# Three edits to the order of work in an encoder block: low parts behind minima, a power behind a weight, another bank for the norm's weights

## The chip, the cores and the metric

The kernel runs on one core of one Trainium2 chip. A core has five engines that run side by side: TensorE (PE, the matmuls, with its weight loads shown apart as PEld), VectorE (DVE), ScalarE (ACT), GpSimd (POOL) and SyncE (SP, which here issues most of the DMAs). Each engine works through its own instructions in the order in which the program holds them; semaphores make one engine wait for another. Matmul results land in PSUM, which has eight banks of 128 partitions x 512 float32; everything else lies in SBUF. The metric is the device time of one execution in microseconds (us), taken as the median of several executions.

## The reference

The program computes one block of an encoder on 1024 tokens of width 1024, with 16 meta tokens ahead of them. All of it is float32:

```python
h = concat([meta, x])                                   # 1040 rows
n = rms_norm(h, norm_mix)                               # y * rsqrt(mean(y*y) + EPS) * gain
qa, ka, va, qb, kb, vb, ga, gb = split(n @ w_in)
y_a = differential_attention(qa, ka, va, ...)           # 4 heads, two softmaxes each, over all keys
y_a = rms_norm(y_a, subln_gain) * (1 - LAMBDA_INIT)     # inside differential_attention, per head
y_b = windowed_gqa(qb, kb, vb, sink_logits)             # 8 heads, keys within 128 tokens and the meta tokens
h = h + (sigmoid(ga) * (y_a @ w_branch_a) + sigmoid(gb) * (y_b @ w_branch_b)) @ w_out
h = h + (silu(f @ w_ff_gate) * (f @ w_ff_up)) @ w_ff_down      # f = rms_norm(h, norm_ffn)
return rms_norm(h, norm_final)[16:]
```

## The kernel before

**Arithmetic.** Nearly every product is made from operands that are split in two: a high part (the value copied into the fp32r type) and a low part (the value minus its high part). A product is then three matmuls: high x high, high x low and low x high. So nearly every matrix that goes into a product needs a copy and a subtraction. Out of PSUM, ScalarE makes the high part (`activation(..., AF.Copy)`) and VectorE the low part (`tensor_tensor(..., ALU.subtract)`); for weights GpSimd makes one or both.

**The stages, in order of time.** First the rows of `x` are normed, turned by TensorE and split into `hT_hi` and `hT_lo`, while the first projections (`kb` and two of `qb`) already run on the columns that are there. Then come the other projections, with the windowed attention ("B") mixed in. From about 268 us the differential attention ("A", lines 1074 to 1161) runs, mixed with the products for the gates (lines 914 to 1031). After that come the two branch products, `w_out`, the feed-forward part and the last norm.

**What sets the order.** A planner orders each engine's instructions by a simulated timeline. Three things bind it. `tc.issue_after(ins)` puts what is written in its block behind `ins` on the engine of `ins`, without a semaphore. `queue_behind` does so for single pairs. And `manual_schedule` keeps the written order: for TensorE from line 1190, for GpSimd from there to line 1226, for all engines in the last stage. So in the first stage, up to about 268 us, TensorE's order too comes from the planner.

**The first stage, around lines 547 to 626.** The weights `norm_mix`, as eight rows of 128, are turned and spread over all partitions by TensorE into two PSUM banks, the list `gain` (lines 560 to 566). The norms of the row tiles 0 and 1 (`norm_x(0, gain)`, `norm_x(1, gain)`) read these banks directly (line 156). For the later tiles the weights are copied into SBUF, `gmix`, by two VectorE copies (`gmix_part`, line 593). Line 549 takes another bank, `idle`, for matmuls on zeros that keep TensorE at work (lines 556 and 569). The banks `pp0`, `pp1` and `pp2` go round (`pp_bank`, line 188): `gain_0` has `pp0`, `gain_1` has `pp1`, the first chunk of `kb` has `pp2`, and then the first chunk of `qb` has `pp0` again. `idle` has the bank `by`, which the windowed attention uses later. The weights of the first `qb` column block are split in `prep` (lines 223 to 230): ScalarE makes the high part (line 224), VectorE one `gmix` half (593), the two halves of the low part (228) and the other `gmix` half (593). Behind the high part ScalarE makes that of a third column block (`q1_h`, line 597), and then squares and sums row tile 2 (line 148, in `norm_x(2)`).

A norm is a chain over three engines: ScalarE squares and sums (148), GpSimd scales the sum and raises it to the power -1/2 (133 and 134), VectorE multiplies by it and by the weights (158). TensorE then turns the result (169), ScalarE and VectorE split it (171 and 173).

**The differential attention.** The loop at line 1200 goes through 32 tiles of 128 queries (4 heads x 8 tiles); a string of slots (line 41) says in which order TensorE gets a piece of the scores ("s"), of the turning of the previous tile ("t"), of the values and the norm ("n"), and a quarter of a gate product ("g"). For each of two softmaxes (`m` = 1, then 0) the scores are made in three chunks (line 1091). The first two lie in the two-bank tile `two`, of which there is one; an instruction on VectorE adds the distances and takes the minimum of both (line 1094, the scores have their sign turned). The third chunk, in one of three banks `sc`, is done by line 1098. ScalarE then takes the exponential (1102), VectorE works out a factor (1105, 1107) and combines both softmaxes (1108). For the tile before, TensorE turns the result in three blocks `b` = 0, 1, 2 (1121), each in a bank `sc`, and each is split by ScalarE (1124) and VectorE (1125).

After every four tiles the values are normed (`normed_a`, 1138): TensorE sums squares (1147), VectorE scales (1151, 1152), GpSimd raises to the power -1/2 (1153), TensorE spreads the factors some slots later (1158).

**The gate products.** `weights_g` (841) makes one operand on GpSimd: for some of them two sums (857, 858), then the copy that is the high part (876) and the subtraction that is the low part (877, kept in the list `made_g`). Each is chained behind the one before. TensorE uses it in four quarters of three matmuls (980). Operands are made up to four products ahead (1031).

Of the kernel before, what the change touches and what calls it, by code (L numbers as in the profile page):

```python
# [79 lines left out]
def encoder_block(ctx: ExitStack, tc: tile.TileContext, x, meta, norm_mix, w_in, lq1, lk1, lq2, lk2,  # L80
# [7 lines left out]
    def f32(ap):  # L88
        return ap.bitcast(F32)
# [13 lines left out]
    def bank(p, tag, name, bufs):  # L103
        return p.tile([P, 512], F32, tag=tag, name=name, bufs=bufs)
# [105 lines left out]
    def prep(col, name, p=None):  # L210
        if col not in raw_w:
            preload(col)
        w = raw_w.pop(col)
        p, bufs = (p, 1) if p else (wpool, W_BUFS)
        wh = p.tile([P, DC, P], F32R, tag="wh", name=f"wh_{name}", bufs=bufs)
        wl = p.tile([P, DC, P], F32R, tag="wl", name=f"wl_{name}", bufs=bufs)
        halves = [slice(4 * b, 4 * b + 4) for b in range(2)]
        if col == C_KB:
            for b in halves:
                nc.gpsimd.tensor_copy(wh[:, b], w[:, b])  # L220
            for b in halves:
                nc.gpsimd.tensor_tensor(wl[:, b], w[:, b], f32(wh)[:, b], ALU.subtract)
        elif col == C_QB:
            high = nc.scalar.activation(wh, w, AF.Copy)
            last = gmix_part(0)
            for b in halves:
                with tc.issue_after(last.ins):
                    last = nc.vector.tensor_tensor(wl[:, b], w[:, b], f32(wh)[:, b], ALU.subtract)
            with tc.issue_after(last.ins):
                gmix_part(1)  # L230
        else:
            split(wh, wl, w, nc.gpsimd)
        return wh, wl
# [312 lines left out]

    zeros = bpool.tile([P, 512], BF16, tag="by1", name="zeros", bufs=2)
    nc.vector.memset(zeros, 0.0)
    idle = bank(psum1, "by", "idle", 1)
    load_x(0)  # L550

    rows = bpool.tile([DC, P], F32, tag="by1", name="gain_rows", bufs=2)
# [6 lines left out]
    nc.vector.tensor_copy(gain_t, pt[:, 0:DC])  # L559
    gain = []  # L560
    for b in range(2):
        pt = pp_bank(f"gain_{b}")
        gain.append(pt)
        for c in range(4):
            k = 4 * b + c
            turned = nc.tensor.transpose(pt[:, c * P:(c + 1) * P], gain_t[:, k:k + 1].broadcast_to([P, P]), ident)
# [21 lines left out]
    q1_h, q1_l = (kvpool.tile([P, DC, P], F32R, tag=tag, name=f"w{tag}") for tag in ("q1", "q0"))  # L588


    def gmix_part(b):
        with tc.issue_after(low.ins):
            return nc.vector.tensor_copy(gmix[:, b * 512:(b + 1) * 512], gain[b])

    with tc.issue_after(highs[-1].ins):
        ensure(2)
        high = nc.scalar.activation(q1_h, w_q1, AF.Copy)
    prepped[C_QB + P] = q1_h, q1_l
    with tc.issue_after(high.ins):
        norm_x(2)  # L600
    with tc.issue_after(normals[-1].ins):
        nc.vector.tensor_tensor(q1_l, w_q1, f32(q1_h), ALU.subtract)
    p_kb = project_steps(C_KB, KB_CHUNKS, "kb", kb_evac, hi_first=True)
# [470 lines left out]
    def scores_a(h, t, ld, s):  # L1074
# [10 lines left out]
        for m in (1, 0):  # L1085
            s[m] = s0s[t % 2] if m == 0 else apool.tile([P, L], F32, tag="s1", name=f"as1_{nm}", bufs=S_BUFS[1])
            two = psum2.tile([P, 2, 512], F32, tag="two", name=f"aps2_{nm}_{m}", bufs=1)
            for i, (k0, n) in enumerate(A_CHUNKS):
                ps = two[:, i] if i < 2 else bank(psum2, "sc", f"aps_{nm}_{m}", SC)
                for vv in range(2):  # L1090
                    nc.tensor.matmul(ps[:, :n], qs[m][:, t * P:(t + 1) * P], ks[m][:, vv, k0:k0 + n],  # L1091
                                     start=(vv == 0), stop=(vv == 1))
                if i == 1:
                    nc.vector.tensor_tensor_reduce(s[m][:, 0:2 * n].rearrange("p (a k) -> p a k", a=2), two[:, :, :n],  # L1094
                                                   dist[:, u0:u0 + 2 * n].rearrange("p (a k) -> p a k", a=2), slope, far_a,
                                                   ALU.add, ALU.min, mn[:, m, 0:1])
# [13 lines left out]
        nc.scalar.copy(more, last)  # L1110
        far_copy(h * NT + t + 2)

    def transpose_a(h, t, s, at_):
        i = t % 2
        for b in range(3):
# [9 lines left out]
            nc.vector.tensor_tensor(lo, pt[:lo.shape[0], :nb], f32(hi)[:lo.shape[0]], ALU.subtract)  # L1125
            yield

    def values_a(h, t, v, at_, py):
# [9 lines left out]
    def normed_a(h, c, py):  # L1138
# [11 lines left out]
        e = small.tile([P, 4], F32, tag="ae", name=f"ae_{nm}", bufs=2)  # L1150
        nc.vector.scalar_tensor_tensor(e, sums, EPS, sums, ALU.mult, ALU.mult)
        nc.vector.scalar_tensor_tensor(f, pst[:, 0:4], 1.0 / P, e, ALU.mult, ALU.add)
        nc.gpsimd.tensor_tensor(f, f, neg_half, ALU.pow)
        for _ in range(N_WAIT):
            yield
        pf = bank(psum2, "sc", f"apf_{nm}", SC)
# [846 lines left out]
```

## Time and profile before

| | us |
|---|---|
| median of the three timed executions | 1407.80 |
| lowest and highest of them | 1406.76 and 1407.81 |
| the profiled execution, device time | 1407.06 |
| its span, first to last instruction | 1405.3 |
| TensorE busy within the span | 1395.5 |
| VectorE busy | 926.8 |
| ScalarE busy | 682.2 |
| GpSimd busy | 661.9 |

The granted TensorE clock was 0.999 over the span. In the profile's timeline a line has the start in us, the duration in us, the engine, the line of the kernel, the operation, its tiles (out<-in), its shape and, in brackets, the idle time of the engine before it with what ended that. The durations of matmuls overlap, because matmuls are pipelined: what TensorE really loses is read from the distance of two starts, beside the usual distance of the same pair. PEld is TensorE's weight load, which runs ahead of the matmul that uses it.

### The profile page before, as it was taken

The page shows a single profiled execution, that of the slowest core. Times are in us where ns is not written, and L with a number is a line of the kernel's source. Part 1 is how long each engine was busy: PE and PEld are TensorE (multiplying, and loading weights), DVE is VectorE, ACT ScalarE, POOL GpSimd, SP SyncE. Part 2 cuts the span into 40 slices and gives each one's busy share as a digit, 9 for nine tenths or more (in the row PEclk, how much of TensorE's full clock was granted, in tenths as well). Part 3 has the DMA queues.
Part 4 walks back from the last instruction along what each step waited for, and adds up shares of the span by engine and source line. Part 5 has one row for each costly group of instructions (what it writes and reads, how often), then busy time and mean ns, then how long its engine had stood idle before and what let it go on. Part 6 is the DMA issues. An engine that isn't in the chain of part 4 may idle for free.

```text
span 1405.3 us, 20672 instructions
## 1 busy us (share of the span) xinstructions
PE 1395.5 (99%) x7169; PEld 1199.8 (85%) x7169; DVE 926.8 (66%) x1594; ACT 682.2 (49%) x1322; POOL 661.9 (47%) x637
## 2 busy tenths in 40 slices
PE   9999999999999999999999999999999999999998
PEld 8989999988888989888888888888888888888886
DVE  7556667676677878657868965644455543887566
ACT  6355565555454656645446644333333333444454
POOL 5347884485686767613404154554455451000442
PEclk9999999999999999999999999999999999999999
DMA  8435658464896363485603534333323324954343
GB/s 235 102 93 169 206 190 285 130 203 137 276 301 219 109 208 106 164 300 165 225 16 140 168 120 146 116 113 113 99 97 112 105 98 135 335 183 142 121 127 143
DMA packets 188601, 226.56 MB, mean 161 GB/s; under 512 B 14584, under 2 KB 122048, under 8 KB 188368
## 3 DMA queue, kind: packets, MB, share of 16 engines
q1 hardware_dynamic: 184736, 219.79, 48.6%
q10 hardware_dynamic: 3760, 5.45, 1.2%
q8 instruction: 57, 0.93, 0.3%
q14 instruction: 48, 0.39, 0.1%
HBM read 152.48 MB, written 68.39 MB: 157 GB/s over the span
## 4 chain that ended last, share of the span: by engine, by line
PE 98%; DVE 1%; ACT 1%; POOL 0%; DMA 0%; issue 0%; ACTq 0%; DVEq 0%; POOLq 0%
PE pg L1765 30%; PE pd L1870 15%; PE pg L980 11%; PE ppa L790 6%; PE aps L1091 4%; PE po L1668 4%; PE apy L1134 3%; PE pp_ka L259 3%; PE pp_va L259 3%; PE pp_qb L259 3%; PE apt L1121 2%; PE bps L449 2%; PE pp_qa L259 2%; PE po L1676 2%; PE bpy L496 1%; PE bpt L490 1%
## 5 line engine op out<-in xcount | busy, mean ns | idle before, releaser
L1765 PE MATMUL pg<-t,wop 128*128 128x512 f32 x1056 | 242.4, 389 | 0.0
L1765 PEld LDWEIGHTS pg<-t,wop 128*128 128x128 f32 x1056 | 198.3, 188 | 41.1
L126 POOL TENSOR_TENSOR wop<-wf,wop 128x512 fp32r<-128x512 f32 x114 | 152.9, 1341 | 162.6 <-ACT wop L125 152.6
L1870 PE MATMUL pd<-ob,oa 128*128 128x512 f32 x924 | 209.6, 389 | 0.0
L1870 PEld LDWEIGHTS pd<-ob,oa 128*128 128x128 f32 x924 | 173.3, 188 | 36.1 <-DVE ob L126 0.2
L1765 PE MATMUL pg<-b,wop 128*128 128x512 f32 x792 | 183.3, 389 | 0.0
L980 PE MATMUL pg<-hT_hi,wopg 128*128 128x512 f32 x488 | 182.1, 400 | 0.3 <-POOL wopg L877 0.3
L1765 PEld LDWEIGHTS pg<-b,wop 128*128 128x128 f32 x792 | 148.5, 188 | 30.7
L125 ACT ACTIVATE wop<-wf 128x512 fp32r<-128x512 f32 x128 | 80.7, 632 | 72.7 <-PE pg L1765 47.7
L126 POOL TENSOR_TENSOR oa<-ra,oa 128x512 fp32r<-128x512 f32 x27 | 35.0, 1296 | 168.6 <-ACT oa L125 167.2
L1102 ACT ACTIVATE as<-as,amn 128x1040 f32<-128x1040 f32 x64 | 74.6, 1166 | 79.9 <-DVE amn L1098 78.6
L980 PEld LDWEIGHTS pg<-hT_hi,wopg 128*128 128x128 f32 x488 | 91.6, 188 | 14.9 <-POOL wopg L877 0.7
L125 ACT ACTIVATE oa<-ra 128x512 fp32r<-128x512 f32 x77 | 48.7, 632 | 108.2 <-PE pd L1870 46.4
L980 PE MATMUL pg<-hT_lo,wopg 128*128 128x512 f32 x244 | 95.8, 393 | 0.0
L1542 DVE TENSOR_TENSOR s<-wf,wf 128x512 f32<-128x512 f32 x22 | 17.4, 793 | 111.2 <-DMA wf<-in_w_ff_up_dram 69.7
L1091 PE MATMUL aps<-ak,aq 128*128 128x352 f32 (+1 forms) x384 | 86.3, 333 | 0.4 <-DVE amn L1094 0.4
L1094 DVE CUSTOM_DVE_ANT_0 as<-aps,dist,far_a 128x704 f32<-128x704 f32 x64 | 60.3, 943 | 20.5 <-PE aps L1091 20.4
L461 POOL TENSOR_SCALAR bs<-bs,bdn 128x432 f32<-128x432 f32 (+1 forms) x64 | 37.1, 599 | 74.9 <-DVE bdn L459 65.4
L1091 PEld LDWEIGHTS aps<-ak,aq 128*128 128x128 f32 x384 | 63.6, 189 | 7.6 <-DVE amn L1094 0.6
L451 DVE CUSTOM_DVE_ANT_0 bs<-bps,tbx,nsink 128x432 f32<-128x432 f32 (+1 forms) x64 | 38.1, 625 | 46.6 <-PE bps L449 24.8
L1792 ACT COPY p<-pg 128x512 f32<-128x512 f32 x44 | 25.9, 588 | 66.4 <-PE pg L1765 64.3
L1134 PEld LDWEIGHTS apy<-at,av 128*128 128x128 f32 x400 | 54.0, 189 | 4.1
(341 smaller groups left out, 3145.7 us busy)
## 6 DMA issues: line engine op xcount, KB each, us to landing
ra<-aop SPq DMA_DIRECT2D x77, 256.0 KB, 2.7
wf<-in_w_ff_gate_dram SPq DMA_DIRECT2D x25, 512.0 KB, 3.8
wf<-in_w_ff_up_dram SPq DMA_DIRECT2D x25, 512.0 KB, 3.7
aop<-as SPq DMA_DIRECT2D x40, 256.0 KB, 2.0
wg_s<-in_w_in_dram SPq DMA_DIRECT2D x18, 512.0 KB, 4.7
ak<-ka_d SPq DMA_DIRECT2D x16, 520.0 KB, 6.5
t_d<-tst SPq DMA_DIRECT2D x16, 512.0 KB, 4.1
wg_f<-in_w_in_dram SPq DMA_DIRECT2D x16, 512.0 KB, 5.2
```

Of the source, the lines that this page charges most:

```text
L125: high = nc.scalar.activation(hi, src, AF.Copy)
L126: lo_eng.tensor_tensor(lo, src, f32(hi), ALU.subtract)
L259: product = nc.tensor.matmul(ps[:, :n], a[:, c, :], b[:, c, at:at + n], start=(u == 0), stop=(u == 3 * DC - 1))
L790: nc.tensor.matmul(ps, w[:, a, j, :], src(j, b, tk), start=(j == 0 and n == 0), stop=(j == 3 and n == 2))
L980: product = nc.tensor.matmul(ps, op[:, x, c, :], h[:, 4 * d + c, HALF[t]], start=(p in (1, 6, 7) and c == 0 and i == 0), stop=(p in (2, 6, ...
L1091: nc.tensor.matmul(ps[:, :n], qs[m][:, t * P:(t + 1) * P], ks[m][:, vv, k0:k0 + n], start=(vv == 0), stop=(vv == 1))
L1094: nc.vector.tensor_tensor_reduce(s[m][:, 0:2 * n].rearrange("p (a k) -> p a k", a=2), two[:, :, :n], dist[:, u0:u0 + 2 * n].rearrange("p ( ...
L1102: nc.scalar.activation(s[m][:, 0:L], s[m][:, 0:L], AF.Exp, bias=mn[:, m, 1:2], scale=-1.0, accum_out=dn[:, 1:2] if m else first_sum)
L1134: nc.tensor.matmul(py[:, cols], v[:kp, a, k, :], at_[:kp, k, b, :], start=(k == 0 and j == 0), stop=(k == 8))
L1668: nc.tensor.matmul(sets_o[p][u], oa[:, a, u * P:(u + 1) * P], ob[:, b, :], start=(p in (1, 5) and j == 0 and k == 0), stop=(p in (2, 3) an ...
L1765: nc.tensor.matmul(ps, op[:, x, c, :], b[:, y, c, :], start=(p in (1, 5) and c == 0 and n == 0), stop=(p in (4, 2, 3) and c == 3 and n == ...
L1870: nc.tensor.matmul(ps[u], oa[:, a, u * P:(u + 1) * P], ob[:, b, :], start=(p in (1, 2, 5) and j == 0 and k == 0), stop=(p in (2, 3, 4) and ...
```

## The change

There are three edits.

**Low parts behind minima.** In `transpose_a`, for the first tile of the first head only, the low parts of blocks 0 and 2 are not issued at once but held in a list. They are issued in `scores_a`, behind the next minimum of line 1094 on VectorE. Block 1 stays as it was.

**A power behind a weight.** The power of line 1153, for the second group of four tiles of the first head only, is put behind the low part of the last but one gate operand that has been made by then (`made_g[-2]`) on GpSimd.

**The first projections.** `idle` takes a bank of the round, `pp0`, and `gain_0` takes the bank `by` in its place; `gain_1` stays in `pp1`. The copy of `gain_1` into `gmix` goes from VectorE to ScalarE, behind the high part of the first `qb` block; the copy of `gain_0` stays on VectorE, but between the two halves of that block's low part. The squares of row tile 2 go ahead of `q1_h` on ScalarE.

```diff
         elif col == C_QB:
             high = nc.scalar.activation(wh, w, AF.Copy)
-            last = gmix_part(0)
+            with tc.issue_after(high.ins):
+                shared = nc.scalar.activation(gmix[:, 512:], gain[1], AF.Copy)
+            last = low
             for b in halves:
                 with tc.issue_after(last.ins):
                     last = nc.vector.tensor_tensor(wl[:, b], w[:, b], f32(wh)[:, b], ALU.subtract)
-            with tc.issue_after(last.ins):
-                gmix_part(1)
+                if not b.start:
+                    with tc.issue_after(last.ins):
+                        last = nc.vector.tensor_copy(gmix[:, 0:512], gain[0])
...
-    idle = bank(psum1, "by", "idle", 1)
+    idle = pp_bank("idle")
...
-        pt = pp_bank(f"gain_{b}")
+        pt = pp_bank(f"gain_{b}") if b else bank(psum1, "by", "gain_0", 1)
...
     with tc.issue_after(highs[-1].ins):
         ensure(2)
-        high = nc.scalar.activation(q1_h, w_q1, AF.Copy)
+        norm_x(2)
+        with tc.issue_after(squares[-1].ins):
+            nc.scalar.activation(q1_h, w_q1, AF.Copy)
     prepped[C_QB + P] = q1_h, q1_l
-    with tc.issue_after(high.ins):
-        norm_x(2)
...
                 if i == 1:
-                    nc.vector.tensor_tensor_reduce(s[m][:, 0:2 * n].rearrange("p (a k) -> p a k", a=2), two[:, :, :n],
+                    least = nc.vector.tensor_tensor_reduce(s[m][:, 0:2 * n].rearrange("p (a k) -> p a k", a=2), two[:, :, :n],
                                                    dist[:, u0:u0 + 2 * n].rearrange("p (a k) -> p a k", a=2), slope, far_a,
                                                    ALU.add, ALU.min, mn[:, m, 0:1])
+                    with tc.issue_after(least.ins):
+                        while held:
+                            held.pop()()
...
             nc.scalar.activation(hi, pt[:kp, :nb], AF.Copy)
-            nc.vector.tensor_tensor(lo, pt[:lo.shape[0], :nb], f32(hi)[:lo.shape[0]], ALU.subtract)
+            def low(lo=lo, of=pt[:lo.shape[0], :nb], hi=f32(hi)[:lo.shape[0]]):
+                return nc.vector.tensor_tensor(lo, of, hi, ALU.subtract)
+            if not h and not t and b != 1:
+                held.append(low)
+            else:
+                low()
             yield
...
-        nc.gpsimd.tensor_tensor(f, f, neg_half, ALU.pow)
+        with tc.issue_after(made_g[-2].ins) if (h, c) == (0, 1) else ExitStack():
+            nc.gpsimd.tensor_tensor(f, f, neg_half, ALU.pow)
```

More of the change, by code (lines that the diff above doesn't have):

```diff
@@ L588, in encoder_block @@
     q1_h, q1_l = (kvpool.tile([P, DC, P], F32R, tag=tag, name=f"w{tag}") for tag in ("q1", "q0"))
-    def gmix_part(b):
-        with tc.issue_after(low.ins):
-            return nc.vector.tensor_copy(gmix[:, b * 512:(b + 1) * 512], gain[b])
     with tc.issue_after(highs[-1].ins):
         ensure(2)
-        high = nc.scalar.activation(q1_h, w_q1, AF.Copy)
+        norm_x(2)
+        with tc.issue_after(squares[-1].ins):
+            nc.scalar.activation(q1_h, w_q1, AF.Copy)
     prepped[C_QB + P] = q1_h, q1_l
-    with tc.issue_after(high.ins):
-        norm_x(2)
     with tc.issue_after(normals[-1].ins):
@@ L1111, in scores_a @@
         far_copy(h * NT + t + 2)
+    held = []
     def transpose_a(h, t, s, at_):
```

## The prediction

> **What bounds the kernel now.** I read the page first, for which engine fills the span; then the busy time by stretches, for where that engine is idle; then what TensorE's weight loads waited for, for what could remove the idle time; and at last the timeline and the chain at each of those places. The page:
>
> ```profile
> span 1405.3 us, 20672 instructions
> PE 1395.5 (99%) x7169; PEld 1199.8 (85%) x7169; DVE 926.8 (66%) x1594; ACT 682.2 (49%) x1322; POOL 661.9 (47%) x637
> ```
>
> TensorE is busy for all but 9.8 us. The next view says where these are (columns: stretch, length, then busy time of PE, PEld, DVE, ACT, POOL with counts).
>
> ```profile
> 0.00:12.00 12.00, 10.17 (x49) 5.93 (x50) 5.66 (x11) 7.24 (x11) 8.23 (x40) 1.00 0.91 276
> 25.00:267.00 242.00, 242.00 (x1506) 226.18 (x1505) 155.06 (x372) 135.31 (x325) 138.26 (x142) 1.00 0.54 163
> 285.00:300.00 15.00, 14.58 (x76) 12.12 (x76) 11.06 (x21) 7.09 (x14) 12.40 (x14) 1.00 0.86 267
> 1398.00:1406.00 8.00, 0.28 (x2) 0.00 (x0) 1.50 (x2) 2.02 (x4) 0.82 (x2) 0.74 0.54 200
> ```
>
> The end, after the last matmul, and the first 12 us hold most of it, and the change touches neither the end nor the loads and norms ahead of the first products. What it can touch is the 0.42 us between 285 and 300 and two more gaps, near 12.6 and 389, which the timelines below show. Busy time understates a loss, since matmuls overlap, so I take distances of starts there. The waits of the weight loads name the later two places, and one wait that I use for a rival (columns: who waited, for whom, us in total, times, longest):
>
> ```profile
> PEld pg L980 <- POOL wopg L877: 0.7, 1, 0.7
> PEld aps L1091 <- DVE amn L1094: 0.6, 1, 0.6
> PEld bpy L487 <- DVE btm L483: 0.5, 1, 0.5
> ```
>
> Each happens once. So the change is worth at most what three short gaps lose, and 0.2% of the time (2.8 us) is about what a measurement of this kernel can tell from no change.
>
> **The first projections.** The timeline, with what TensorE, VectorE and ScalarE do:
>
> ```profile
> 10.63 1.05 ACT L224 ACTIVATE wh_c<-w_c 128x1024 fp32r<-128x1024 f32 x1
> 11.91 0.68 DVE L593 COPY gmix<-gain 128x512 f32<-128x512 f32 x1
> 12.26 0.28 PE L259 MATMUL pp_kb<-hT_hi,wl_c 128*128 128x256 f32 x1
> 12.38 0.28 PE L259 MATMUL pp_kb<-hT_lo,wh_c 128*128 128x256 f32 x1
> 12.74 0.36 PE L259 MATMUL pp_qb<-hT_hi,wh_c 128*128 128x256 f32 x1
> 17.48 1.28 DVE L158 SCALAR_TENSOR_TENSOR xn_a<-x,rstd_a,gmix 128x1024 f32<-128x1024 f32 x1 [0.45 <-POOL rstd_a L134]
> 19.16 0.27 PE L169 MATMUL ptn_a<-ident,xn_a 128*128 128x128 f32 x1
> ```
>
> ```profile
> 16.03 1.42 POOL L134 TENSOR_TENSOR rstd_a<-rstd_a,neg_half 128x1 f32<-128x1 f32 x1
> 18.90 0.55 POOL L134 TENSOR_TENSOR rstd_a<-rstd_a,neg_half 128x1 f32<-128x1 f32 x1
> ```
>
> Two matmuls of this width start 0.12 us apart (12.26 and 12.38), so `qb` should have started at 12.50 and started at 12.74. Its weights were ready at 11.68 (10.63 + 1.05). The bank `pp0` was read by the VectorE copy until 12.59 (11.91 + 0.68), and that came last of what `qb` needs. With `idle` in `pp0` and `gain_0` in `by`, no reader stands ahead of `qb`: it starts at 12.50. Gain 0.24 us; nothing else writes `by` for some time, and the first half of `qb`'s low part comes earlier, the second half as late as now, since one copy still stands ahead of it.
>
> What is added is one copy out of PSUM on ScalarE. Its nearest row is the copy of the other half on VectorE, 0.68 us; I take that, and no less than none. It delays what comes behind it on ScalarE by at most itself: the squares of tile 2 go ahead of `q1_h` and don't suffer, those of tile 3 may come up to 0.68 us later. Tile 3's norm ends at 18.76 (17.48 + 1.28), and TensorE turns it at 19.16: 0.40 us of cover. If all of the delay passed through, the part would cost 0.28 us instead. But the chain has more cover ahead of that: the power of tile 3 (16.03) took 1.42 us and the next one 0.55, so 0.87 us of it went by on something that is not the squares, and a delay of 0.68 fits in there. So I take no loss. This part: -0.24 us, between -0.24 and +0.28.
>
> **The low parts.** Three starts on TensorE, the same pair elsewhere without a wait, the chain through VectorE, and GpSimd's line at that time:
>
> ```profile
> 296.98 0.40 PE L980 MATMUL pg<-hT_hi,wopg 128*128 128x512 f32 x1
> 297.40 0.66 PE L1121 MATMUL apt<-ident,as 128*128 128x128 f32 x4
> 298.46 0.92 PE L1091 MATMUL aps<-ak,aq 128*128 128x352 f32 x4 [0.40 <-DVE amn L1094]
> ```
>
> ```profile
> 379.86 0.39 PE L980 MATMUL pg_True<-hT_hi,wopg_True 128*128 128x512 f32 x1
> 380.09 0.60 PE L1121 MATMUL apt<-ident,as 128*128 128x128 f32 x4
> 380.44 0.89 PE L1091 MATMUL aps<-ak,aq 128*128 128x352 f32 x4
> ```
>
> ```profile
> 291.23 0.69 DVE at L1125
> 291.92 0.86 DVE as L1094
> ...
> 295.14 1.60 DVE as L1108
> 296.75 0.79 DVE at L1125 x2
> 297.54 0.86 DVE as L1094
> ```
>
> ```profile
> 289.81 0.89 PE L1091 MATMUL aps<-ak,aq 128*128 128x352 f32 x4
> 294.36 1.29 POOL L858 TENSOR_TENSOR wg_f<-wg_f,wg_f 128x512 f32<-128x512 f32 x1
> ```
>
> The usual distances are 0.23 us (379.86 to 380.09) and 0.35 us (380.09 to 380.44). So the scores should have started at 296.98 + 0.23 + 0.35 = 297.56 and started at 298.46: 0.90 us lost in all, 0.19 before the turning (it waits for the bank that the low part of block 1 reads) and 0.71 before the scores (they wait for the minimum at 297.54, which frees `two`).
>
> What is late ahead of it? The minimum at 291.92 stood behind the low part of block 0. The scores it needs ended at 290.70 (289.81 + 0.89). With block 0 held it starts near 290.74, and the low part takes its place behind it, 0.69 us. Minimum and low part are then through at 290.74 + 0.86 + 0.69 = 292.29, against 291.92 + 0.86 = 292.78 now, and line 1098, the exponential and the factor follow some 0.5 us earlier, 0.7 at most if line 1098 starts with less of a gap behind a low part than behind a minimum. So line 1108 starts between 294.4 and 294.65 instead of at 295.14. At the other end, block 2's low part goes behind the minimum: of the 0.79 us for both, 0.69 is block 1, 0.10 to 0.19 the other (the busy times overlap by about 0.08). So the minimum comes about 0.15 us earlier even if nothing else does.
>
> Whether that arrives is decided by GpSimd. Here line 1108 took 1.60 us, and its median over the run is 1.30:
>
> ```profile
> L1108 DVE SCALAR_TENSOR_TENSOR as<-as,adn,as x32: 1286/1302/2447, 284.8 to 574.9; 128x1040 f32<-128x1040 f32 x32
> ```
>
> GpSimd's subtraction ran from 294.36 to 295.65, and line 1108 ended at 296.74, 1.09 us after that: it made hardly any headway before. The Trainium skill's page "SBUF — State Buffer", section "SBUF: two separate sides", has a rule for this: VectorE with two SBUF inputs and GpSimd compete for one pair of ports, the one that starts first has it for its whole instruction, and "the other fully blocks". The row agrees with it; by that rule too the start decides between the two sums below. At 294.4 or later, line 1108 comes behind the start of the subtraction (294.36), waits until 295.65 and ends at 296.74 as before. Then only the 0.15 us are won. At 294.3 it would come first, end by 295.7 and leave block 1 (0.69) and the minimum (0.86) done by 297.25, ahead of 297.56: then all 0.90 us are won. The two orders are 0.1 us apart and my working is no better than 0.2 us, but my numbers put GpSimd first. I take -0.15 us, between 0 and -0.90. If VectorE comes first, the subtraction is late by about 1.1 us; no wait of a gate product shows near it (the one in the list of waits is at 389), so I take that as covered, and 1.1 us less what is won if it is not.
>
> Cost of holding: the bank of block 0 is freed some 0.4 us later (292.3 instead of 291.92); no wait shows there. Nothing else is added: the low parts are moved, not made anew.
>
> **The power.** GpSimd and TensorE:
>
> ```profile
> 380.37 1.30 POOL L858 TENSOR_TENSOR wg_f<-wg_f,wg_f 128x512 f32<-128x512 f32 x1
> 384.86 2.08 POOL L1153 TENSOR_TENSOR af<-af,neg_half 128x4 f32<-128x4 f32 x1 [3.19 <-DVE af L1152]
> 386.90 0.61 POOL L876 CAST wopg<-wg_f 128x512 fp32r<-128x512 f32 x1
> 387.58 1.29 POOL L877 TENSOR_TENSOR wopg<-wg_f,wopg 128x512 fp32r<-128x512 f32 x1
> ```
>
> ```profile
> 388.22 0.40 PE L980 MATMUL pg<-hT_lo,wopg 128*128 128x512 f32 x1
> 388.92 0.73 PE L980 MATMUL pg<-hT_hi,wopg 128*128 128x512 f32 x2 [0.31 <-POOL wopg L877]
> ```
>
> The third matmul of the product (7, 6) takes the low part and should have started at 388.45; it started at 388.92: 0.47 us lost. That low part was made last, behind the power, which had GpSimd idle for 3.19 us. Counted through the four products made ahead, `made_g[-1]` at that point is the operand (7, 2) and `made_g[-2]` is (7, 6), just the one that TensorE waits for. Its source was ready at 381.67 (380.37 + 1.30). So its copy and subtraction run from there, 0.61 + 1.29 us, until about 383.6, 5 us before they are used, and the power still starts when its input comes, at 384.86. What is queued behind it are the operands of (7, 2), which stand behind it now as well. Gain -0.47 us, between 0 and -0.5; a delay of the power would reach TensorE only at the spreading of the factors:
>
> ```profile
> 393.44 0.60 PE L1158 MATMUL apf<-ident,af 128*128 128x128 f32 x4
> ```
>
> That is 6.5 us after its end at 386.94.
>
> **Sum.** -0.24 - 0.15 - 0.47 = -0.86 us. Against the profiled execution (1407.06) that is 1406.2; the median of the three timed ones is 0.74 above it (1407.80). The four executions lie at 1406.76, 1407.06, 1407.80 and 1407.81, mean 1407.36; from that I forecast 1406.5.
>
> **Rivals.** (1) VectorE comes first near 294.3: 0.90 instead of 0.15, sum -1.61, 1405.75. For it: only 0.1 us separate the orders, and GpSimd waits for loads here, whose times move on their own. Against: my estimate of 294.4 to 294.65. (2) Slower. The first part changes what the planner simulates, and TensorE's order from 12 to 267 us is the planner's. That stretch now has no idle time at all in 242 us, so another order can only add. The price of one unit placed too early is the kind of wait that the `bpy` row shows, 0.5 us. From two such waits on the gain of 0.86 is gone; with four the time is 1407.36 - 0.86 + 2.0 = 1408.5. Against: priorities follow the program's text, which hardly moves. (3) The power doesn't do what it says, because the copy at 386.90 waited for something else that ended by then, a buffer or a load: sum -0.39, 1407.0. Against: 3.19 us of idle time, then the copy without a gap.
>
> **How the numbers follow.** Forecast 0.48, rival 1 0.27, rival 2 0.15, rival 3 0.10. For the range I take the lowest execution with rival 1's sum, 1406.76 - 1.61 = 1405.15, rounded to 1405.0, and at the top the highest with half of rival 2, 1407.81 - 0.86 + 1.25 = 1408.2. Faster by over 0.2% would need 2.8 us, more than all three places lose: 0.04, for an order that happens to be better by itself. Slower by over 0.2% needs more than seven waits of 0.5 us: 0.04. The rest, 0.92, is the same.
>
> **What would show it.** Right: `qb` starts 0.12 us after the last `kb` matmul near 12.5; the minimum of the second tile stands ahead of block 0's low part near 290.5; the wait for line 877 near 389 is gone, and the power follows a subtraction. Whether line 1108 starts before or after line 858 tells the forecast from rival 1. Wrong: idle time of TensorE between 12 and 267 us, another order of `kb`, `qb` and the turnings there, or a time outside 1405.0 to 1408.2.

## The result and the profile after

| | us |
|---|---|
| before, median of 21 executions (lowest, highest) | 1407.64 (1406.76, 1408.90) |
| after, median of 21 executions (lowest, highest) | 1404.97 (1404.24, 1409.07) |
| ratio with its 95% interval | 0.9981 [0.9975, 0.9987] |
| profiled execution of after, device time and span | 1405.68 and 1403.9 |

The change takes 2.67 us off, about 0.19% (0.13% to 0.25% by the interval). The forecast of 1406.5 took off 0.86, and the low end of its range, 1405.0, lies just above the measured median. So the direction was right, and the sum was a third of what came.

The page of after, to stand against that of before (span 1405.3, PE 1395.5):

```profile
span 1403.9 us, 20673 instructions
PE 1395.7 (99%) x7169; PEld 1200.3 (85%) x7169; DVE 925.7 (66%) x1593; ACT 682.2 (49%) x1323; POOL 660.0 (47%) x637
```

TensorE's work is the same; its idle time in the span fell from 9.8 to 8.2 us. The busy time by stretches says where (stretch, length, then PE, PEld, DVE, ACT, POOL with counts):

```profile
0.00:12.00 12.00, 10.42 (x47) 6.16 (x48) 5.69 (x11) 7.27 (x11) 8.21 (x40) 1.00 0.93 274
25.00:267.00 242.00, 242.00 (x1510) 226.24 (x1508) 154.78 (x372) 135.49 (x325) 138.40 (x142) 1.00 0.55 163
285.00:300.00 15.00, 14.69 (x77) 12.29 (x76) 12.04 (x23) 7.49 (x15) 12.39 (x14) 1.00 0.82 259
```

Between 25 and 267 us TensorE is as full as before. Between 285 and 300 it gained 0.11 us of busy time, and the waits of the weight loads fit that: the wait for line 877 near 389 is gone. Of the two near 297 the one for the minimum (`aps`) is shorter, 0.4 instead of 0.6, and the one for a low part (`apt`) is 0.5 as before.

```profile
PEld apt L1125 <- DVE at L1130: 0.5, 1, 0.5
PEld pd L1880 <- DVE ob L126: 0.4, 1, 0.4
PEld aps L1090 <- DVE amn L1093: 0.4, 1, 0.4
```

That does not add up to 2.67 us. One trace of each kernel turned out to be too few, because executions of one kernel differ at these very places. So here are three traces of each, and of the other kernels below. For each TensorE instruction I took its start minus that of the same instruction in the first trace of before; the median in a stretch is how far the kernel is behind (negative: ahead) by then. The last two columns are the time from the start of the last matmul to the end of the span, and the span.

```
                by 285   300-380  400-480  520-580  700-1190  1250-1395   end    span
before            0.00     0.00     0.00     0.00      0.00      0.00     7.37   1405.26
before_look      -0.53    -0.10    -0.12     0.51      0.56      0.51     7.38   1405.78
before_look2      0.09     0.48     0.48     1.24      1.26      1.21     7.37   1406.47
after            -0.30    -0.41    -1.03    -0.88     -0.88     -0.61     6.60   1403.89
after_look       -0.14    -0.36    -0.98    -1.03     -0.95     -0.73     6.61   1403.77
all_again        -0.23    -1.19    -1.81    -1.90     -2.00     -1.99     6.60   1402.50
a_low            -0.14    -1.09    -1.10    -1.18     -1.15     -1.20     7.37   1404.06
b_power          -0.06    -0.00    -0.62    -0.45     -0.45     -0.50     6.74   1404.13
c_first          -0.23    -0.48    -1.07    -1.16     -1.22     -1.27     6.58   1403.20
c_pinned         -0.12    -0.10    -0.14     0.66      0.66      1.53     6.71   1406.13
fetch_moved      -0.15     0.48     0.45     0.44      0.49      0.44     6.81   1405.14
sum_late         -0.26    -1.18    -1.80    -1.92     -1.99     -2.03     6.59   1402.45
sum_out          -0.06     0.49     0.46     0.74      0.70      0.68     6.57   1405.14
```

The means of three traces (before, before_look, before_look2 against after, after_look, all_again) differ by 2.45 us in the span, close to the 2.67 of the medians. By place, as the difference of what each kernel gains from column to column: -0.08 by 285 us, -0.70 near 297 (low parts), -0.61 near 389 (power), -0.46 near 513, -0.03 from there to 1190, +0.20 near 1200, and -0.77 at the end, behind the last matmul. The prediction had the second and third of these, and nothing at 513 or at the end.

**The first projections.** What TensorE, ScalarE and VectorE do there in after:

```profile
11.40 0.28 PE L262 MATMUL pp_kb<-hT_lo,wh_c 128*128 128x256 f32 x1
11.54 0.59 ACT L226 ACTIVATE gmix<-gain 128x512 f32<-128x512 f32 x1
11.70 1.01 PEld L262 LDWEIGHTS pp_qb<-hT_hi,wh_c 128*128 128x128 f32 x8 [0.23 <-ACT wh_c L224]
11.70 1.22 PE L262 MATMUL pp_qb<-hT_hi,wh_c 128*128 128x256 f32 x8
12.46 1.06 ACT L148 ACTIVATE xn_a<-x 128x1024 f32<-128x1024 f32 x1 [0.33 <-DMA x<-in_x_dram]
17.43 1.31 DVE L158 SCALAR_TENSOR_TENSOR xn_a<-x,rstd_a,gmix 128x1024 f32<-128x1024 f32 x1 [0.45 <-POOL rstd_a L134]
```

`qb` no longer waits for the bank. But it no longer stands behind `kb` either: the planner put it in the middle of `kb`'s products, at 11.70, where it waits for ScalarE's high part (0.30 us from 11.40 to 11.70, 0.12 without a wait). The copy on ScalarE took 0.59 us and was through at 12.13; the squares behind it waited for their load until 12.46 anyway, so it cost nothing. Tile 3's norm ends at 18.74, as before (18.76).

**The low parts.** VectorE and GpSimd, first in the profiled execution of after, then in another one (all_again):

```profile
290.44 0.95 DVE L1093 CUSTOM_DVE_ANT_0 as<-aps,dist,far_a 128x704 f32<-128x704 f32 x1 [0.31 <-PE aps L1090]
291.31 0.69 DVE L1130 TENSOR_TENSOR at<-apt,at 128x512 fp32r<-128x512 f32 x1
...
292.77 1.29 POOL L856 TENSOR_TENSOR wg_f<-wg_f 128x512 f32<-128x512 f32 x1 [0.97 <-DMA wg_f<-in_w_in_dram]
...
294.11 2.42 DVE L1110 SCALAR_TENSOR_TENSOR as<-as,adn,as 128x1040 f32<-128x1040 f32 x1
294.14 1.29 POOL L857 TENSOR_TENSOR wg_f<-wg_f,wg_f 128x512 f32<-128x512 f32 x1
...
295.50 1.50 POOL L875 CAST wopg<-wg_f 128x512 fp32r<-128x512 f32 x1
...
297.06 0.93 DVE L1093 CUSTOM_DVE_ANT_0 as<-aps,dist,far_a 128x704 f32<-128x704 f32 x1
```

```profile
293.24 1.30 POOL L856 TENSOR_TENSOR wg_f<-wg_f 128x512 f32<-128x512 f32 x1 [2.16 <-DMA wg_f<-in_w_in_dram]
...
294.15 1.49 DVE L1110 SCALAR_TENSOR_TENSOR as<-as,adn,as 128x1040 f32<-128x1040 f32 x1
294.61 2.18 POOL L857 TENSOR_TENSOR wg_f<-wg_f,wg_f 128x512 f32<-128x512 f32 x1
...
296.16 0.94 DVE L1093 CUSTOM_DVE_ANT_0 as<-aps,dist,far_a 128x704 f32<-128x704 f32 x1
```

The order is what the edit asks for: minimum at 290.44, low part behind it. Then there are two outcomes in one and the same kernel. In the first GpSimd's second sum has its 1.29 us and line 1110 takes 2.42; in the second line 1110 takes 1.49 and the sum 2.18, and the next minimum starts 0.90 us earlier. What differs most ahead of them is when the load of GpSimd's operand landed: its first sum starts at 292.77 or at 293.24, and line 1110 at 294.11 or 294.15.

**The power.** GpSimd in after:

```profile
379.96 1.29 POOL L857 TENSOR_TENSOR wg_f<-wg_f,wg_f 128x512 f32<-128x512 f32 x1
381.31 0.61 POOL L875 CAST wopg<-wg_f 128x512 fp32r<-128x512 f32 x1
382.00 1.30 POOL L876 TENSOR_TENSOR wopg<-wg_f,wopg 128x512 fp32r<-128x512 f32 x1
383.25 0.61 POOL L875 CAST wopg<-wg_f 128x512 fp32r<-128x512 f32 x1
384.45 2.08 POOL L1163 TENSOR_TENSOR af<-af,neg_half 128x4 f32<-128x4 f32 x1 [0.60 <-DVE af L1161]
```

The copy and the subtraction of (7,6) now stand in the 3.19 us in which GpSimd sat idle before, and TensorE's wait is gone.

**The end.** The DMA view of the last store, from 4.6 to 6.3 us behind the last matmul's start, first of before (packets, MB, share of 16 engines):

```profile
q10 hardware_dynamic: 92, 0.16, 25.9%
q1 hardware_dynamic: 36, 0.04, 7.0%
q14 instruction: 1, 0.01, 1.1%
```

The same stretch in after, and then 2.4 us earlier in after:

```profile
q10 hardware_dynamic: 93, 0.16, 24.8%
q1 hardware_dynamic: 34, 0.04, 6.1%
```

```profile
q10 hardware_dynamic: 142, 0.26, 41.8%
q1 hardware_dynamic: 81, 0.13, 22.4%
q14 instruction: 1, 0.01, 1.1%
```

The queue q14 carries no data of the kernel: it is a packet of 8192 bytes of instruction code. In before it starts 5.0 us behind the last matmul's start and takes 0.31 us, in the midst of the last store; two packets of that store then take 0.285 and 0.216 us instead of some 0.085, and the store's last large packet ends at 6.05 us. In after the code packet comes at 2.76 us, and the store's last large packet ends at 5.34. The last two stores are issued at the same moments in both kernels, 2.92 and 2.94 us behind the matmul's start. They take 3.4 and 3.6 us from issue to landing in before, 2.5 and 2.8 us in after. The earlier packet of after makes the store ahead of them longer (2.8 us instead of 2.0), and nothing waits for that one.

### The profile page after: what moved, and what is told of

It is laid out like the page before. It is cut to its first block, busy times and chain, and to the rows that moved or that the text cites. A ratio compares the mean times of both kernels' runs of the same rounds, so it can differ in the third digit from the quotient of the medians.

```text
span 1403.9 us, 20673 instructions
## 1 busy us (share of the span) xinstructions
PE 1395.7 (99%) x7169; PEld 1200.3 (85%) x7169; DVE 925.7 (66%) x1593; ACT 682.2 (49%) x1323; POOL 660.0 (47%) x637
## 4 chain that ended last, share of the span: by engine, by line
PE 99%; DVE 1%; ACT 0%; issue 0%; ACTq 0%; DVEq 0%
PE pg L1775 30%; PE pd L1880 15%; PE pg L979 12%; PE ppa L789 6%; PE aps L1090 4%; PE po L1678 4%; PE apy L1143 3%; PE pp_ka L262 3%; PE pp_va L262 3%; PE pp_qb L262 3%; PE apt L1125 2%; PE bps L452 2%; PE pp_qa L262 2%; PE po L1686 2%; PE bpy L499 1%; PE bpt L493 1%
```

## The experiments

Three theories stood against each other in the first group. P: each part brings what the prediction gave it, and the rest is scatter. L: VectorE comes first near 294 in most executions, so that the low parts bring far more. T: the extra comes at the end. The ratios below are worked out over the executions and not from the two medians, so the two can differ a little. The expectations count the end from the end of the last matmul, the table from its start, which is 0.39 us more.

**a_low: the low parts alone.** Only the hunks of `scores_a` and `transpose_a`:

```diff
+                    with tc.issue_after(least.ins):
+                        while held:
+                            held.pop()()
...
+            if not h and not t and b != 1:
+                held.append(low)
```

> Only the low parts behind minima. Theory P (the prediction's prices, and the rest of the measured 2.7 us is scatter between executions): -0.15 us, and line 1108 of the second tile ends behind GpSimd's subtraction. Theory L (the ports: in most executions VectorE comes first, unlike in the profiled one): about -0.9 us or more, with line 1108 ending about 1.1 us earlier. Theory T (what is gained beyond the three places comes at the end of the kernel, from the last waits and the store): -0.15 us up to the branch products, whatever the total.

Measured 1406.80 against 1407.78, ratio 0.9996 [0.9987, 1.0005]. In its trace VectorE comes first, and TensorE is 0.95 us further ahead behind 297 than before it. The end is 7.37 us, as in before. So the low parts can bring all of the 0.90 us that the prediction named, and they do nothing at the end.

**b_power: the power alone.**

```diff
+        with tc.issue_after(made_g[-2].ins) if (h, c) == (0, 1) else ExitStack():
+            nc.gpsimd.tensor_tensor(f, f, neg_half, ALU.pow)
```

> Only the power behind a weight. Theories P and L: -0.47 us, the wait for line 877 near 389 gone, nothing else moved. Theory T: -0.47 us up to the branch products and possibly more at the end.

Measured 1405.96, ratio 0.9990 [0.9981, 0.9999], 1.82 us below before. TensorE gains 0.62 us at 389, as in after, and 0.63 us come at the end, which is 6.74 instead of 7.37 us. An edit near 385 us has moved the code packet near the end, here to 7.10 us, behind the last store: the planner issues some of SP's DMAs in another order, and SP's instructions change with that. The remaining 0.57 is well within the interval.

**c_first: the first projections alone.** The hunks of lines 222 to 600.

> Only the first projections. Theories P and L: -0.24 us at the first transposition of row tile 2, no more later. If the changed order of TensorE in the first 60 us is worth something by itself, the gain grows between there and 268 us; by theory T the total can be larger than the gain at the branch products.

Measured 1405.52, ratio 0.9989 [0.9980, 0.9997], 2.26 us below before, far more than any of P, L and T gave it. The trace shows why: TensorE is only 0.23 us ahead by 285 us, but then gains 0.25 near 297 and 0.59 near 389, places that this part doesn't touch, and its end is 6.58. The later orders have changed: the minimum of the second tile stands ahead of block 0's low part, and the copy of (7,6) ahead of the power, the very orders that the two other edits ask for:

```profile
290.51 0.95 DVE L1093 CUSTOM_DVE_ANT_0 as<-aps,dist,far_a 128x704 f32<-128x704 f32 x1 [0.31 <-PE aps L1090]
291.38 0.69 DVE L1124 TENSOR_TENSOR at<-apt,at 128x512 fp32r<-128x512 f32 x1
...
381.25 0.61 POOL L875 CAST wopg<-wg_f 128x512 fp32r<-128x512 f32 x1
384.38 2.07 POOL L1152 TENSOR_TENSOR af<-af,neg_half 128x4 f32<-128x4 f32 x1 [2.52 <-DVE af L1151]
```

An edit of the first stage was enough for the planner to choose them; the timeline that it simulates is not on record. This is also why the parts don't add up (0.98, 1.82 and 2.26 alone, 2.69 together).

**all_again: after once more, on the same chip.**

> The changed kernel once more, for a second trace. Theory P: as its profile, -0.9 us at the branch products and -1.4 us at the end. Theory L: line 1108 of the second tile ends 1.1 us earlier than in the first trace, and the branch products start about 1.6 us earlier than before. Theory T: -0.9 us at the branch products, and the end differs between the two traces.

Measured 1405.09 against 1407.78, ratio 0.9981 [0.9972, 0.9990], 2.69 us. Its trace is the second one shown above for the low parts, with VectorE first.

**c_pinned: the first projections with the two later orders held as before.** Beside the hunks of c_first:

```diff
+                    with tc.issue_after(lows[-1].ins) if lows and len(lows) <= 3 else ExitStack():
                         nc.vector.tensor_tensor_reduce(...)
...
+        power = nc.gpsimd.tensor_tensor(f, f, neg_half, ALU.pow)
+        if (h, c) == (0, 1):
+            queue_behind([copies_g[-2]], power)
```

> The first-projections edit alone, with two orders held as they were before: the minimum of line 1094 stays behind the low part of block 0, and the copy of (7,6) stays behind the power. Replanning theory: what the edit alone showed beyond some 0.2 us came from later orders that the planner changed with it. So here TensorE is 0.1 to 0.3 us earlier than before at the first projections, keeps that and wins nothing near 297 and nothing near 389; the span behind the last matmul is 7.0 or 6.2 us, whichever way the code fetch falls. Time 1407.5 with the long end, 1406.8 with the short one. Rival, the first stage itself is worth more (its new order of TensorE): 1406.2 or less, with TensorE already 0.5 us or more ahead at 268 us.

Measured 1407.20 against 1407.94, ratio 1.0000 [0.9991, 1.0008]. TensorE is 0.12 us ahead by 285 us and wins nothing near 297 or 389; the end is 6.71. So the part by itself is worth some 0.1 us, and what c_first showed beyond that and the end came from the two later orders. The rival (0.5 us or more by 268 us) falls. Its trace also loses 0.80 us near 513 and 0.87 near 1200, where it waits for a load and for VectorE.

**fetch_moved: before with three more DMA issues on SP.** The load of `nfin` goes in four pieces; the trace has the same instructions in the same order on every other engine.

```diff
-            nc.sync.dma_start(nfin, norm_final.rearrange("(o n) -> o n", o=1).broadcast_to([P, D]))
+            for c in range(0, D, 256):
+                nc.sync.dma_start(nfin[:, c:c + 256], norm_final[c:c + 256].rearrange("(o n) -> o n", o=1).broadcast_to([P, 256]))
```

> The kernel before with one load (nfin, some 20 us ahead of its use) issued in four pieces, which puts a few more instructions on SP ahead of the last stores and changes nothing else. Fetch theory: the 0.7 to 0.8 us at the end are lost where a block of instruction code is fetched over the last store's packets, and its place follows the number of SP's instructions. So here the end behind the last matmul falls from 7.0 to 6.2 or 6.3 us, TensorE's times stay, and the time is 0.7 us below before: 1407.0. Rival, the end's length comes from what the change does to stores or to the last norm: the end stays at 7.0 and the time within 0.2 of before.

Measured 1406.94 against 1407.94, ratio 0.9992 [0.9984, 1.0001]. The end is 6.81 instead of 7.37 us, a little less of a gain than expected, and the code packet is now at 2.73 us, ahead of the last store, whose last large packet ends at 5.31. The stretch from 4.6 to 6.3 us has no code packet any more:

```profile
q10 hardware_dynamic: 100, 0.17, 27.1%
q1 hardware_dynamic: 39, 0.05, 7.8%
```

So the end is shown to hang on where the code packet falls, and a change of SP's instructions alone is shown to move that packet. The interval of the time alone would not settle it; the trace does. SP's recorded instructions fit: 1226 in before and in a_low, the two kernels with the long end, and another number in each kernel with a short one (1222 in after, 1227 in b_power, 1229 here). But the number does not give the place: b_power and sum_out both have 1227, and their packets come at 7.10 and 2.73 us. Which engine's code the packet holds, and how its moment follows from SP's instructions, no trace shows.

This kernel's trace says something more of before's order near 297, where it lost 0.63 us more than the first trace of before did:

```profile
293.46 1.30 POOL L857 TENSOR_TENSOR wg_f<-wg_f 128x512 f32<-128x512 f32 x1 [1.10 <-DMA wg_f<-in_w_in_dram]
294.83 1.30 POOL L858 TENSOR_TENSOR wg_f<-wg_f,wg_f 128x512 f32<-128x512 f32 x1
294.99 2.24 DVE L1108 SCALAR_TENSOR_TENSOR as<-as,adn,as 128x1040 f32<-128x1040 f32 x1
```

The load landed 0.47 us later than in the trace that the prediction read (292.99), GpSimd came first again, and line 1108 ended 0.49 us later (297.23 instead of 296.74). TensorE was 0.15 us ahead at 285 us, so against it the load was later still.

**sum_late: after with GpSimd held back.** A memset between the two sums of operand (3,6):

```diff
             tt(a21, a21, a22, ALU.add)
+            if (k, p) == (3, 6):
+                op = operand()
+                nc.gpsimd.memset(f32(op)[:, 0], 0.0)
             tt(a21, a21, a11, ALU.subtract)
```

> The kernel after with one GpSimd memset of 128x512 between the two sums of operand (3,6), so that the second sum starts near 294.7 to 295.1 instead of 294.1 to 294.6. Port theory: VectorE's line 1110 then starts first in every execution, takes 1.3 to 1.5 us instead of up to 2.4, and all of 0.90 us is won near 297. The median falls below after by what the executions with GpSimd first had lost, 0.2 to 0.6 us: 1404.4 to 1404.9. Prediction's theory (GpSimd's sum isn't what decides): line 1110 as before, time as after. Rival on the other side: the operand (3,6) is some 1.5 us later, and TensorE waits for it: 0.5 us or more above after.

```profile
292.68 1.29 POOL L861 TENSOR_TENSOR wg_f<-wg_f 128x512 f32<-128x512 f32 x1 [1.05 <-DMA wg_f<-in_w_in_dram]
293.91 0.52 POOL L864 MEMSET wopg<- 128x512 f32 x1
294.15 1.30 DVE L1119 SCALAR_TENSOR_TENSOR as<-as,adn,as 128x1040 f32<-128x1040 f32 x1
294.39 2.21 POOL L865 TENSOR_TENSOR wg_f<-wg_f,wg_f 128x512 f32<-128x512 f32 x1
```

The load landed earlier than in any other trace, which in after means that GpSimd comes first. Here VectorE's line (1119 in this kernel, 1110 in after) came first and took 1.30 us, and TensorE gained 0.92 us near 297. So the order of these two instructions is what decides about that place, and GpSimd's sum being 1.2 us later (it ended at 296.60, in after at 295.43) costs nothing. The time doesn't show it: 1404.96 against 1407.94, ratio 0.9982 [0.9973, 0.9991], no less than after's 1404.97, and not within the 1404.4 to 1404.9 expected. The profiled execution (1404.33) was the fastest of its eleven, and what the others lost, no trace shows. This version is not faster than after by anything that was measured.

**sum_out: before with the first of GpSimd's sums left out.** The computation lacks that sum for one operand, and the power of line 1153 is held behind the copy of (7,6) with the `queue_behind` of c_pinned, as it stands in before.

```diff
+            if (k, p) != (3, 6):
+                tt(a21, a21, a22, ALU.add)
             tt(a21, a21, a11, ALU.subtract)
```

> The kernel before without the first of the two sums on GpSimd for operand (3,6) (this sum is left out of the computation), so that the subtraction of line 858 starts with the load's landing, near 293, and is through by 294.3, ahead of line 1108. The order of VectorE stays as before. Port theory: line 1108 then takes 1.3 us from 294.6 to 295.1, and the minimum behind it comes 0.4 to 0.9 us earlier; of what the low parts' edit won, that much was GpSimd's. Time 0.4 to 0.9 us below before: 1407.1 to 1407.5. Rival, line 1108's long time isn't GpSimd's: it stays at 1.6 to 2.2 us, the time at 1407.9.

```profile
294.85 1.29 POOL L878 TENSOR_TENSOR wopg<-wg_f,wopg 128x512 fp32r<-128x512 f32 x1
295.08 2.16 DVE L1109 SCALAR_TENSOR_TENSOR as<-as,adn,as 128x1040 f32<-128x1040 f32 x1
```

Measured 1407.24 against 1407.72, ratio 0.9993 [0.9984, 1.0001]. The time fell into the range that I gave the port theory, but not for its reason: line 1108 (1109 here) took 2.16 us, as the rival said, and TensorE lost 0.55 us more near 297. The experiment was badly laid: with one sum less, GpSimd's next two-input instruction, the low part of the same operand, moved up to 294.85 and stood in the way instead. The gain is the end again (6.57), since SP's order had changed. What it adds is one more collision of another instruction with the same result.

**before_look, after_look and before_look2: more traces.**

> The kernel before, looked at once more, for where its executions differ by 0.5 us or more. If it is the loads: a stage in the middle is longer, at a wait for a load; the end behind the last matmul is 7.0 us again and line 1108 again comes behind GpSimd's sum. If it is the end: the end's length differs between executions of one kernel.

> The kernel after, looked at a third time. If the order of GpSimd's second sum and line 1110 hangs on when the load of operand (3,6) lands: with a landing that starts the first sum after about 293.0, VectorE comes first, line 1110 takes 1.3 to 1.5 us and TensorE's wait near 296 is gone; with an earlier landing GpSimd comes first, 2.3 to 2.4 us. The end behind the last matmul is 6.2 us either way.

> The kernel before, looked at a third time. Line 1108 comes behind GpSimd's second sum again, and ends some 2.4 us after that sum's start, so that its end follows the load's landing; the end behind the last matmul is 7.0 us. A wait for the keys' load near 513 is there in some executions and not in others (0.5 us in the second look, none in the first); if so, it and the landing near 293 are what executions of one kernel differ by.

They took 1407.93, 1405.65 and 1408.39 us. The ends are 7.38, 6.61 and 7.37, so the end belongs to the kernel and not to the execution. In after_look the first sum starts at 292.82 and GpSimd comes first (line 1110: 2.30 us), as expected of an early landing. In before_look2 the first sum starts at 293.45 and line 1108 ends at 297.22. Both further traces of before wait near 513 for the keys of the next head, the third one most:

```profile
PEld aps L1091 <- DMA ak<-ka_d: 0.8, 1, 0.8
```

From the issue to the landing these loads took 10.0 us there (median in the DMA view) and 8.9 us in the first trace of before, which doesn't wait.

## Why the prediction was wrong, step by step

**What bounds the kernel.** "The change touches neither the end nor the loads and norms ahead of the first products": this is the step that failed, for the end. It brought 0.77 us, as much as my whole sum less 0.09. I had looked for what the edits do to the instructions at the end, and there they do nothing. What they do is to change the order, and with it the number, of SP's instructions, and a block of code is then fetched at another moment. fetch_moved shows that SP's instructions by themselves can move it; that it was they in after too, where other engines' orders also change, is inferred. The Trainium skill's page "Runtime: NRT & Kernel Launch", section "Instruction fetch mechanics", says that an engine's sequencer fetches its code by a DMA queue of its own and that the cost of a block's boundary is mostly hidden. The traces show code on queues apart from the data's, without naming an engine; and in the last store the cost was not hidden: the end is 0.56 to 0.80 us longer with the packet there (7.37 against 6.57 to 6.81).

**The missing 1.59 us.** The sum was 0.86 and the traces' means differ by 2.45. The end brought 0.77 of what is missing, the low parts 0.55, the place near 513 0.46, the power 0.14, and 0.03 came up to 1190 us; against that the first projections brought 0.16 less than forecast, and 0.20 was lost near 1200.

**First projections: -0.24 forecast, -0.06 to -0.17 measured.** So much TensorE gains between its first `kb` products and 60 to 200 us in the six traces with this part (c_pinned 0.13). Of the seven with before's first stage, one (before_look2) loses 0.12 there and the others don't move. The means by 285 us differ by less, 0.08, because before_look alone lacks some waits near 220 us, 0.5 us in all. Bank and copy went as argued. "It starts at 12.50", behind `kb`, was wrong: rival 2's sign, another order of `kb` and `qb`, was there, at a price of 0.18 us at 11.70 and nothing later. And the cover of the copy on ScalarE was another than I named: the squares waited for their load.

**Low parts: -0.15 forecast, -0.70 in the mean of three traces.** The mechanism was right, and the term mis-sized. With GpSimd first, after and after_look gained 0.11 and 0.22 us at that place, just the 0.15 of the forecast; with VectorE first, all_again gained 0.96, rival 1's 0.90. My error was to hold GpSimd's 294.36 fixed and to put VectorE's 294.4 to 294.65 against it. Both ends moved. VectorE was ready at 294.11 to 294.28. That is earlier than my estimate only because TensorE was ahead by then: with its lead at 285 us added back, it is 294.38 to 294.42 in all six traces with this order. GpSimd's first sum started anywhere from 292.68 to 293.46 over twelve traces, with its load. Which one comes first fits whether VectorE is ready before GpSimd's first sum ends: it ended at 294.06 (after), 294.11 (after_look) and 294.02 (c_first) where VectorE came second, and at 294.54 (all_again) and 294.48 (a_low) where VectorE came first. And I took before's loss, 0.90, as a constant. In before line 1108 ends with GpSimd's sum, so a load that is late against TensorE makes before slower and lets VectorE win in after. Two of three traces of before lost 0.4 us more that way: in before_look2 the first sum started 0.46 us later, in before_look 0.09 earlier but with TensorE 0.53 ahead.

**Power: -0.47 forecast, -0.62 in all three traces of after.** `made_g[-2]` was (7,6), the copy filled the gap, and nothing behind the power waited. Of the 0.15 beyond the forecast, 0.1 stands at the matmul after the third, whose start I hadn't taken into the distance.

**Not forecast: -0.46 near 513 and +0.20 near 1200.** Two of three traces of before wait for the keys' load near 513, and after's three hardly do (0.15 at most). c_pinned, with before's order near 297 and 389, loses 0.80 there, and fetch_moved, with before's orders throughout, nothing. So the wait comes and goes with the execution. Over all thirteen traces five of the seven with before's order near 297 lose 0.17 to 0.80 us there, and none of the six with the new order more than 0.15. Whether after is less prone to it stays open: it issues the first of these loads 1.0 to 1.9 us earlier than the first trace of before, but its TensorE is ahead by as much. The wait for `ob` near 1200 comes and goes too (0.27 us in after, 0.22 in after_look, none in all_again).

**The rivals.** Rival 1 happened in one of three traces of after. Of rival 2 came the other order, at 0.18 us and not at 0.5 a wait, and rival 3 didn't happen. No rival said that a change of order at one place moves orders or code fetches at another, and that was worth more than any single term. The chance of 0.92 for "within 0.2%" fits the -0.19%, but for a sum with a different make-up; and the execution on which I based the terms (1407.06) was a fast one of before, 0.6 below its median, with the load landing early for its TensorE and no wait for the keys.

## What to carry to other kernels

A kernel whose order is planned by a program answers to a local edit everywhere: before a gain is put down to the edit, hold the later orders as they were (c_pinned) or compare the instructions engine by engine. Where an end is tied to a transfer's landing, one trace is one sample: look at three before the loss is taken as a constant. And read the DMA queues behind the last compute instruction: the last store is alone on the path there, and what falls on it, even 8 KB of code, counts nearly in full (here 0.71 us of the store, 0.77 of the end).

## What the runs showed of the hardware

**At this place two-input instructions of VectorE and GpSimd exclude each other to the end.** Where GpSimd came first, VectorE's instruction ended 1.09 to 1.10 us after GpSimd's in ten of ten traces, whether it had started 0.03 us before it (after: 295.43 and 296.53) or 0.78 after (before: 295.65 and 296.74; fetch_moved: 296.13 and 297.23; sum_out, against another GpSimd instruction: 296.14 and 297.24). The other way round, GpSimd's sum ended 1.15 to 1.16 us after VectorE's (all_again: 295.64 and 296.79; a_low and sum_late alike). There line 1110 had waited as well, for GpSimd's first sum: it ended 1.10 us after that one (all_again: 294.54 and 295.64; a_low: 294.48 and 295.59) and so got in between the two sums. This agrees with the rule that the prediction quoted from the Trainium skill's page "SBUF — State Buffer", section "SBUF: two separate sides". But "the one that starts first" cannot be read from the start in the profile: line 1110 shows a start 0.03 us ahead of GpSimd's sum and still came second. GpSimd's one-input copy seems to be held too: the copy at 295.50 in after took 1.50 us instead of the 0.61 of the one at 381.31, and it ended 0.47 us behind line 1110.

**A code packet holds up a store's data packets.** Beside a block of 8192 bytes, which took 0.31 us of packet time, two packets of the last store took 0.285 and 0.216 us instead of some 0.085, and the store's last large packet ended 0.71 us later (6.05 against 5.34 us). That they shared a DMA engine is likely, but the traces give queues and not engines.
